# Sums of the quarters of x by adding DMAs, with the first half of x held negative, and a new order at the beginning of a decoder block kernel

## The chip, the cores and the metric

The kernel runs on one core of a Trainium2 chip. A core has TensorE (PE, matrix products into PSUM), VectorE (DVE), ScalarE (ACT), GpSimd (POOL) and SyncE (SP), each with its own instruction queue, and 16 DMA engines that SP, ACT and POOL give work to. The metric is the device time of one execution in microseconds (us), as the median of several runs. Before the change it is 1400.37 us.

## The reference

One decoder block over x of 1024 positions and 1024 channels, in float32. What matters here is its first step: the RMSNorm of x and the combined input projection.

```python
h = rms_norm(x, mix_norm_g[layer])          # x * rsqrt(mean(x*x) + eps) * g
proj = h @ w_in[layer]                      # 1024 x 5888
z_a, q, k, v, gate_logits = jnp.split(proj, splits, axis=-1)
y_a = chunked_spatial_gating(gelu(z_a), ...)
q, k = partial_rope(q), partial_rope(k)     # needs cos and sin of positions
```

Attention, gates, output projection and the convolutional feed-forward follow; the change touches none of them. The inputs are random, positions run from 0 to 1023.

## The kernel before, in words

**Products in parts.** Each float32 operand is split in a high part, rounded by ACT to float32r, and a low part, the difference, made by DVE. A product of two blocks is three matmul passes (high-high, high-low, low-high). A matmul instruction handles 128 inner channels and 512 positions.

**The input projection by Strassen-Winograd.** x is kept transposed: tile `X` has 8 rows of 128 channels (`kt` 0 to 7) by 1024 positions. Its four quarters are A11 (`kt` 0-3, first 512 positions), A12 (`kt` 4-7, first half), A21 (`kt` 0-3, second half) and A22. `quarter(i, j, kt)` names a row of one: `i` the half of positions, `j` the half of channels. Weights come in pairs of 128 columns (`wr` tiles, two per pair). From pair 2 on, each pair is done with seven block products instead of eight, in the order P1, P2, P6, P7, P5, P4, P3 for pair 2. Their left sides are A11, A12, S2, S3, S1, A22 and S4, with

```
S1 = A21 + A22    S2 = S1 - A11    S3 = A11 - A21    S4 = A12 - S2
```

`x_sum` (L442-450) makes them in place in X: S1 and S2 on DVE, S3 and S4 on POOL, one 128x512 row at a time. `parts_of` and `in_left` (L393-419) split them into the arenas R, G0 and G1, where they stay for all pairs. P2 adds to P1's PSUM bank, P4 to P7's and P3 to P5's; the first value has to be copied out before the second product starts. Pair 2 is evicted to tile C2 by `in_product` (L475-523).

**The first two pairs without the sums.** So that TensorE can start before the norm is known, pairs 0 and 1 multiply the raw x (scaled by the channel gains only, `raw_left`, L429-440) with plain products: `product(n, h, i, k)` is pair n, half h of the positions, column tile i, half k of the channels: 12 matmuls. Their results get the norm factor later, when V is turned (`turn_v`, L595-612). `plain_op` splits the weights, `plain_final` evicts.

**The norm.** `load_rows(h)` loads x by rows into C2 and YC, `square_row` squares them on ACT with a running sum, `root` makes the factor on POOL, `diagonal` (L378) writes it on four diagonals on DVE, `spread` multiplies these with ones on TensorE (`rs_bc`), and `scale_x` (L439) scales X in place.

**The rotation tables.** `rot_tables` (L2146) gives a chain of some 50 small DVE steps (run by `some(n)`), two sines, 16 widening copies on ACT (`wide`), and `turns`: transposes on TensorE and evictions into YC.

**Order.** In `beginning()` (L1024-1125) and through the first seven products, ACT, DVE and TensorE run strictly in the order in which the code calls them. POOL and the DMA queues are placed by the scheduler; each queue runs its own list in order. `meanwhile(i)` (L1127) adds work after product i: S3's parts after P1, S1's after P2, S4's after P7, and then X is released and its memory becomes V, into which the turned blocks of pairs 0 to 2 are evicted. `in_ahead` loads weights and prepares operands ahead.

Of the kernel before, what the change touches and what calls it, by code (L numbers as in the profile page):

```python
# [16 lines left out]
ALU = mybir.AluOpType  # L17
# [76 lines left out]
def block_kernel(  # L94
# [48 lines left out]
    def two(arena, row):  # L143
        return arena[:, row, :].rearrange("p (a t) -> p a t", a=2)
# [197 lines left out]
    for k in range(2):  # L342
        ks = slice(k * QK, (k + 1) * QK)
        nc.sync.dma_start(raws[0, 0][:, ks], w_in[0][:, ks])
        load_x(0, range(k * QK, (k + 1) * QK))
    in_load(0, 1)
    in_load(1, 0)
    load_rows(0)
    in_load(1, 1)
    load_x(1, range(KT))  # L350

    nc.vector.memset(mhalf, -0.5)
    nc.vector.memset(ones, 1.0)
# [16 lines left out]
    def root(h):  # L370
        me = small.tile([P, 4], F32, name=f"me_x{h}", tag="me4", bufs=2)
        rs = rss[h] = small.tile([P, 4], F32, name=f"rs_x{h}", tag="rs4", bufs=2)
        nc.gpsimd.tensor_scalar(me, mss[h], 1.0 / D, EPS, ALU.mult, ALU.add)
        nc.gpsimd.tensor_tensor(rs, me, mhalf.to_broadcast([P, 4]), ALU.pow)

    dgs = [C[1][:, i, upper] for i in range(2)]

    def diagonal(h):  # L378
        for b in range(4):
            dg = dgs[h][:, b * P : (b + 1) * P]  # L380
            nc.vector.tensor_scalar(dg, ident, rss[h][:, b : b + 1], None, ALU.mult)

    def spread(h):
        bc = tr_tile(f"rs_bc{h}")
# [5 lines left out]
    def quarter(i, j, kt):  # L390
        return X[:, j * QK + kt, (lower, upper)[i]]

    def in_left(name, kt, src):  # L393

        arena, row = IN_ROWS[name]
        t = left[name, kt] = two(arena, row + kt)
        return (
            lambda: nc.scalar.activation(t[:, 0], src, AF.Copy),
            lambda: nc.vector.tensor_tensor(t[:, 1], src, f32(t[:, 0]), ALU.subtract),
        )  # L400

    def staggered(items, beside=()):

        beside = list(beside)
        late = None
        for first, hi, lo in items:
            first()
            hi()
            if late:
                late()  # L410
            late = lo
            if beside:
                for fn in beside.pop(0):
                    fn()
        late()

    def parts_of(name, i, j):
        staggered((lambda: None, *in_left(name, kt, quarter(i, j, kt))) for kt in range(QK))

    U_ROWS = {(0, 0): (R, 0), (0, 1): (R, 8), (1, 0): (G1, 0), (1, 1): (R, 12)}
    raw_x = {}

    def raw_left(h, kt):
# [12 lines left out]
        xs = x_half(kt, h)  # L438
        nc.vector.scalar_tensor_tensor(xs, xs, chan[:, kt : kt + 1], bc, ALU.mult, ALU.mult)  # L439

    def x_sum(n, kt):
        a11, a12, a21, a22 = (quarter(i, j, kt) for i in range(2) for j in range(2))  # L442
        if n == 1:
            nc.vector.tensor_tensor(a22, a21, a22, ALU.add)
        elif n == 2:
            nc.vector.tensor_tensor(a11, a22, a11, ALU.subtract)
        elif n == 3:
            nc.gpsimd.tensor_tensor(a21, a11, a21, ALU.subtract)
        else:
            nc.gpsimd.tensor_tensor(a12, a12, a11, ALU.subtract)  # L450


    def c_half(n, i, h):
# [84 lines left out]
    def plain_step(n, h, i, k, kt):  # L538

        if (n, h, i) not in plain_banks:  # L540
            name = f"pl_{n}_{h}_{i}"
            plain_banks[n, h, i] = (
                ps_d.tile([P, HALF], F32, name=name, tag="dn") if i else acc_tile(name)
            )
        acc = plain_banks[n, h, i]
        for p, (w, a) in enumerate(PASSES):
            nc.tensor.matmul(  # L547
                acc, plain_ops[n, k, i][:, w, kt, :], raw_x[h, k * QK + kt][:, a, :],
                start=k == 0 and kt == 0 and p == 0,
                stop=k == 1 and kt == QK - 1 and p == 2,  # L550
                skip_group_check=True,
            )

    def plain_final(n, h, i):
        nc.scalar.activation(c_half(n, i, h), plain_banks[n, h, i], AF.Copy)
# [468 lines left out]
    def beginning():  # L1024

        chain, wide, turns = rot_tables(
            nc, lent, [[C[2][:, i, lower], C[2][:, i, upper]] for i in range(2)],
            acc_tile, ident, positions, YC,
        )
# [12 lines left out]

        def raw_parts(h, kt):
            for fn in raw[h, kt]:
                fn()

        def product(n, h, i, k):
            for kt in range(QK):
                plain_step(n, h, i, k, kt)

        warm_up(12)
        some(5)
        for k in range(2):
            weight(0, k, 0)
            for kt in range(k * QK, (k + 1) * QK):
                raw_parts(0, kt)
            product(0, 0, 0, k)
        some(2)
        weight(0, 0, 1)
        weight(0, 1, 1)  # L1060
        some(4)
        weight(1, 0, 0)
        weight(1, 1, 0)
        plain_final(0, 0, 0)
        for k in range(2):
            product(0, 0, 1, k)
        some(10)
        for b in range(4):
            square_row(0, b)
        load_rows(1)  # L1070
        root(0)
        plain_final(0, 0, 1)
        diagonal(0)
        for k in range(2):
            product(1, 0, 0, k)
        bc0 = spread(0)
        weight(1, 0, 1)
        weight(1, 1, 1)
        for kt in range(KT):
            raw_parts(1, kt)  # L1080
            scale_x(0, kt, bc0)
            some(1)
        plain_final(1, 0, 0)
        for b in range(4):
            square_row(1, b)
        root(1)
        for k in range(2):
            product(1, 0, 1, k)
        some(99)
        plain_final(1, 0, 1)  # L1090
        diagonal(1)
        product(0, 1, 0, 0)
        bc1 = spread(1)
        parts_of("A11", 0, 0)
        product(0, 1, 0, 1)
        parts_of("A12", 0, 1)
        for fn in wide:
            fn()
        for kt in range(KT):
            scale_x(1, kt, bc1)  # L1100
        plain_final(0, 1, 0)
        for k in range(2):
            product(0, 1, 1, k)
        plain_final(0, 1, 1)
        parts_of("A22", 1, 1)
        for kt in range(QK):
            x_sum(1, kt)
            x_sum(3, kt)
        in_ahead(0, 9, 2)
        turns[0]()  # L1110
        for k in range(2):
            product(1, 1, 0, k)
        turns[1]()
        plain_final(1, 1, 0)
        turns[2]()
        for k in range(2):
            product(1, 1, 1, k)
        turns[3]()
        plain_final(1, 1, 1)
        staggered(  # L1120
            (lambda kt=kt: x_sum(2, kt), *in_left("S2", kt, quarter(0, 0, kt)))
            for kt in range(QK)
        )
        for kt in range(QK):
            x_sum(4, kt)

    def meanwhile(i):  # L1127
        if i == 0:
            parts_of("S3", 1, 0)
        elif i == 1:  # L1130
            parts_of("S1", 1, 1)
        elif i == 3:
            parts_of("S4", 0, 1)
            x_stack.close()
            zv["pool"] = zv_stack.enter_context(
                tc.tile_pool(name="zvp", bufs=1, reuse_waits="tile")
            )
# [9 lines left out]
    beginning()  # L1147
# [1133 lines left out]
```

## Time and profile before

| | |
|---|---|
| runs | 1398.46, 1401.39, 1400.37 us; median 1400.37 |
| profiled execution | 1402.62 us, span 1400.9 us |
| TensorE busy | 1368.6 us, 98% of the span |
| VectorE, ScalarE, GpSimd busy | 1036.8, 653.5, 314.8 us |
| granted TensorE clock | 0.993 on average |

The span runs from the first to the last recorded instruction; the execution's own time holds a little more around it. Busy times count compute instructions, not waits or DMA issues. In a timeline row stand start, duration, engine, line of the code, operation, what it writes and reads, its shape, how many, and in brackets the idle time before it with what ended it. `pl` are the plain products, `in_P` the Strassen products, `rs_bc` the spreads, `rot` the table transposes and `vt` the turns of V. In a row of DMA issues stand the count, the size of each and the median us from issue to landing.

### The profile page before, as it was taken

The numbers are of one execution on the slowest core, as the hardware profiler recorded it, in microseconds if no ns is written. First come the engines' busy times: TensorE is split into PE (matmuls) and PEld (weight loads), VectorE is DVE, ScalarE is ACT, GpSimd is POOL, SyncE is SP. The second block draws the span as 40 slices with busy tenths as digits, with TensorE's granted clock in tenths as the row PEclk, the third lists the DMA queues.
The fourth block names the chain that finished last, engine by engine and source line by source line (L and its number), as shares of the span: only waits on it lengthen the run. The fifth ranks groups of instructions, "written<-read, shape, count | busy, mean of one in ns | idle before, by whom it ended". The sixth has DMA issues, their size and how long they took to land.

```text
span 1400.9 us, 19244 instructions
## 1 busy us (share of the span) xinstructions
PE 1368.6 (98%) x6434; PEld 1133.3 (81%) x6434; DVE 1036.8 (74%) x1878; ACT 653.5 (47%) x1285; POOL 314.8 (22%) x305
## 2 busy tenths in 40 slices
PE   9789999999999999999999998999999999999997
PEld 7667888888888788888888877888888888888886
DVE  7978677676876987867889877667666667685674
ACT  7573255555553332634646443334333335454444
POOL 0312000000231000120001147555665554000003
PEclk9999999999999999999999999999999999999999
DMA  9014535354435997694842133223333326997563
GB/s 364 13 49 128 174 105 170 106 166 140 137 104 185 324 310 266 199 313 142 285 130 104 38 113 106 105 93 109 108 105 120 115 74 248 380 318 233 195 211 121
DMA packets 142788, 234.92 MB, mean 168 GB/s; under 512 B 13664, under 2 KB 57440, under 8 KB 142688
## 3 DMA queue, kind: packets, MB, share of 16 engines
q1 hardware_dynamic: 141248, 231.53, 49.4%
q10 hardware_dynamic: 1440, 2.16, 0.4%
q8 instruction: 51, 0.84, 0.2%
q14 instruction: 49, 0.40, 0.1%
HBM read 167.77 MB, written 64.29 MB: 166 GB/s over the span
## 4 chain that ended last, share of the span: by engine, by line
PE 83%; DVE 7%; DMA 4%; issue 3%; ACT 2%; POOL 1%; SPq 0%; POOLq 0%; DVEq 0%; ACTq 0%
PE in_P L486 23%; PE uP L1762 19%; PE dn L2016 11%; PE up L1762 8%; PE pa L1234 5%; PE wo_P L1595 4%; PE pl L547 2%; PE pu L827 2%; PE pu L1741 2%; PE pb L1234 2%; DMA wd<-in_w_down_dram 1%; DMA dS<-gS 1%; PE pp L811 1%; DVE G L166 1%; PE sc L772 1%
## 5 line engine op out<-in xcount | busy, mean ns | idle before, releaser
L486 PE MATMUL in_P<-R,G 128*128 128x512 f32 x1008 | 245.7, 396 | 6.1 <-ACT C L506 4.4
L486 PEld LDWEIGHTS in_P<-R,G 128*128 128x128 f32 x1008 | 186.5, 189 | 43.8 <-ACT C L506 4.8
L2016 PE MATMUL dn<-R 128*128 128x512 f32 x924 | 209.6, 389 | 0.0
L2016 PEld LDWEIGHTS dn<-R 128*128 128x128 f32 x924 | 173.5, 188 | 35.9
L165 ACT ACTIVATE G<-wr 128x512 fp32r<-128x512 f32 x126 | 79.0, 629 | 153.3 <-PE in_P L486 113.3
L165 ACT ACTIVATE R<-up 128x512 fp32r<-128x512 f32 x130 | 79.1, 628 | 123.1 <-PE uP L1762 42.4
L1762 PE MATMUL uP<-G,R 128*128 128x512 f32 x504 | 123.1, 393 | 4.6 <-POOL R L166 2.6
L486 PE MATMUL in_P<-G,G 128*128 128x512 f32 x504 | 123.2, 394 | 1.1 <-DVE C L513 0.8
L1762 PE MATMUL uP<-R 128*128 128x512 f32 x504 | 121.4, 390 | 1.0 <-POOL R L166 1.0
L1762 PE MATMUL up<-G,R 128*128 128x512 f32 x504 | 121.2, 391 | 0.0
L1762 PEld LDWEIGHTS uP<-G,R 128*128 128x128 f32 x504 | 95.4, 190 | 25.3 <-POOL R L166 3.0
L1762 PEld LDWEIGHTS uP<-R 128*128 128x128 f32 x504 | 94.8, 188 | 21.2 <-POOL R L166 1.5
L1762 PEld LDWEIGHTS up<-G,R 128*128 128x128 f32 x504 | 94.6, 188 | 20.5
L486 PEld LDWEIGHTS in_P<-G,G 128*128 128x128 f32 x504 | 92.7, 188 | 20.5 <-issue 1.9
L166 DVE TENSOR_TENSOR G<-wr,G 128x512 fp32r<-128x512 f32 x126 | 90.1, 716 | 20.9 <-ACT G L165 20.9
L166 POOL TENSOR_TENSOR R<-up,R 128x512 fp32r<-128x512 f32 x58 | 88.5, 1526 | 75.6 <-ACT R L165 75.6
L165 ACT ACTIVATE R<-db 128x512 fp32r<-128x512 f32 x77 | 48.1, 626 | 56.3 <-PE dn L2016 46.7
L166 DVE TENSOR_TENSOR R<-up,R 128x512 fp32r<-128x512 f32 x72 | 60.7, 845 | 17.0 <-ACT R L165 17.0
L166 DVE TENSOR_TENSOR R<-db,R 128x512 fp32r<-128x512 f32 x77 | 53.8, 703 | 25.7 <-ACT R L165 25.5
L1234 PE MATMUL pa<-R,G 128*128 128x512 f32 x288 | 67.9, 389 | 0.0
L878 POOL TENSOR_TENSOR ld<-ld,w 128x256 f32<-128x256 f32 x16 | 11.2, 718 | 236.7 <-DVE w L866 236.7
L1234 PEld LDWEIGHTS pa<-R,G 128*128 128x128 f32 x288 | 54.1, 188 | 11.2
(273 smaller groups left out, 2469.4 us busy)
## 6 DMA issues: line engine op xcount, KB each, us to landing
wr<-in_w_in_dram SPq DMA_DIRECT2D x45, 512.0 KB, 4.0
up<-in_w_up_dram SPq DMA_DIRECT2D x44, 512.0 KB, 3.5
dA<-gd SPq DMA_DIRECT2D x55, 256.0 KB, 5.1
wd<-in_w_down_dram SPq DMA_DIRECT2D x44, 256.0 KB, 5.6
wT<-wd SPq DMA_DIRECT2D x44, 256.0 KB, 3.3
dS<-gS SPq DMA_DIRECT2D x44, 256.0 KB, 4.2
db<-wT SPq DMA_DIRECT2D x44, 256.0 KB, 4.3
gd<-Y SPq DMA_DIRECT2D x42, 256.0 KB, 2.0
```

The costliest lines, as they stand in the source:

```text
L165: nc.scalar.activation(hi, src, AF.Copy)
L166: fn = lambda: lo_eng.tensor_tensor(lo, src, f32(hi), ALU.subtract)
L486: nc.tensor.matmul(acc, op[:, w, kt, :], left[LEFT[name], kt][:, a, :], start=opened and kt == 0 and i == 0, stop=kt == QK - 1 and i == 2, ...
L547: nc.tensor.matmul(acc, plain_ops[n, k, i][:, w, kt, :], raw_x[h, k * QK + kt][:, a, :], start=k == 0 and kt == 0 and p == 0, stop=k == 1 ...
L772: nc.tensor.matmul(dst, self.qa[:, h, :], keys, start=True, stop=False)
L811: nc.tensor.transpose(pp[:, i * P : (i + 1) * P], self.pr[:, h, s * P : (s + 1) * P], ident)
L827: nc.tensor.matmul(pu[:, h * HD : (h + 1) * HD], self.pT[:, i, :], vt[:, h * HD : (h + 1) * HD], start=i % n == 0, stop=i % n == n - 1,)
L1234: nc.tensor.matmul(acc, unit[a][kt // 4][:, kt % 4, :], two(R, 8 * h + kt)[:, b, :], start=n == 0 and i == 0, stop=n == len(kts) - 1 and i ...
L1595: nc.tensor.matmul(acc, left[LEFT[name], kt][:, a, blk * P : (blk + 1) * P], out_ops[s][:, w, :], start=name not in SHARED and kt == 0 and ...
L1741: nc.tensor.matmul(acc, plain_up[which, k][:, w, kt, :], left[f"A{h + 1}{k + 1}", kt][:, a, :], start=n == 0 and i == 0, stop=n == KT - 1 ...
L1762: nc.tensor.matmul(acc, op[:, w, kt, :], left[LEFT[name], kt][:, a, :], start=opened and kt == 0 and i == 0, stop=kt == QK - 1 and i == 2, ...
L2016: nc.tensor.matmul(accs[blk], dops[s][:, 0, a, blk * P : (blk + 1) * P], dops[s][:, 1, w, :], start=SEQ[j] not in CONTINUES and kt == 0 an ...
```

## The change

- **Adding DMAs.** `x_sum(n, k)` is now one DMA from the POOL queue for two rows of 512 positions on all partitions (512 KB), which adds its source to its target. S1 is made in `Z`, a view of YC: two plain DMAs on the SP queue, inside the loop of `scale_x(1, ...)`, copy A21 there, then A22 is added. S3 is made over A21, S2 over A11, S4 over A12. There are eight adding DMAs. In the built program POOL's list is S1, S3, S1, S3, S2, S2, S4, S4.
- **Sign.** An adding DMA can't subtract, so the first half of X is scaled by the negative factor (`diagonal(0)`). The parts of A11, A12, S3 and S4 are negated when they are split (`NEGATED`), with a scale of -1 on ACT and a multiply-subtract on DVE.
- **Order.** The second half of x is loaded before the rows and before the weights of pair 1. All plain products of pair 0 come first, for both halves of positions, then those of pair 1. Sixteen chain steps stand between pair 1's weight splits and the first diagonal. The second diagonal is made by ACT. Operands of the first four Strassen products are prepared before the last plain products, and the rest of the chain and the sines come after them.
- **Tables.** The widened tables lie in YC, so they wait until S1's parts are made; their transposes run after the fifth product's second turn, in the PSUM banks of the turns of V (`tr_tile`), where they were among the last plain products in the accumulators' banks.
- **Places.** `U_ROWS` moves the raw parts to other rows of the arenas.

The diff, cut to its core:

```diff
     in_load(0, 1)
+    load_x(1, range(KT))
+    load_rows(0)
     in_load(1, 0)
-    load_rows(0)
-    in_load(1, 1)
-    load_x(1, range(KT))
...
     def diagonal(h):
         for b in range(4):
-            dg = dgs[h][:, b * P : (b + 1) * P]
-            nc.vector.tensor_scalar(dg, ident, rss[h][:, b : b + 1], None, ALU.mult)
+            dg, rs = dgs[h][:, b * P : (b + 1) * P], rss[h][:, b : b + 1]
+            if h == 0:
+                nc.vector.tensor_scalar(dg, ident, rs, -1.0, ALU.mult, ALU.mult)
+            else:
+                nc.scalar.activation(dg, ident, AF.Copy, scale=rs)
...
+    NEGATED = ("A11", "A12", "S3", "S4")
     def in_left(name, kt, src):
         arena, row = IN_ROWS[name]
         t = left[name, kt] = two(arena, row + kt)
+        if name in NEGATED:
+            return (
+                lambda: nc.scalar.activation(t[:, 0], src, AF.Copy, scale=-1.0),
+                lambda: nc.vector.scalar_tensor_tensor(
+                    t[:, 1], src, -1.0, f32(t[:, 0]), ALU.mult, ALU.subtract
+                ),
+            )
...
+    Z = YC.rearrange("p i (a t) -> p (i a) t", a=2)
...
-    U_ROWS = {(0, 0): (R, 0), (0, 1): (R, 8), (1, 0): (G1, 0), (1, 1): (R, 12)}
+    U_ROWS = {(0, 0): (R, 4), (0, 1): (R, 12), (1, 0): (G1, 0), (1, 1): (G0, 4)}
...
-    def x_sum(n, kt):
-        a11, a12, a21, a22 = (quarter(i, j, kt) for i in range(2) for j in range(2))
-        if n == 1:
-            nc.vector.tensor_tensor(a22, a21, a22, ALU.add)
-        elif n == 2:
-            nc.vector.tensor_tensor(a11, a22, a11, ALU.subtract)
-        elif n == 3:
-            nc.gpsimd.tensor_tensor(a21, a11, a21, ALU.subtract)
-        else:
-            nc.gpsimd.tensor_tensor(a12, a12, a11, ALU.subtract)
+    def x_sum(n, k):
+        def q(i, j):
+            kt = j * QK + 2 * k
+            return X[:, kt : kt + 2, (lower, upper)[i]]
+        dst, src = {
+            1: (Z[:, 2 * k : 2 * k + 2], q(1, 1)), 3: (q(1, 0), q(0, 0)),
+            2: (q(0, 0), Z[:, 2 * k : 2 * k + 2]), 4: (q(0, 1), q(0, 0)),
+        }[n]
+        nc.gpsimd.dma_start(dst, src, accum_op=ALU.add)
...
         plain_final(0, 0, 0)
+        product(0, 0, 1)
+        for kt in range(KT):
+            raw_parts(1, kt)
+        product(0, 1, 0)
+        plain_final(0, 0, 1)
         for b in range(4):
             square_row(0, b)
         load_rows(1)
+        in_load(1, 1)
         root(0)
+        weight(1, 0, 0)
+        weight(1, 1, 0)
+        plain_final(0, 1, 0)
+        some(16)
         diagonal(0)
+        product(0, 1, 1, (0,))
         bc0 = spread(0)
+        product(0, 1, 1, (1,))
         for kt in range(KT):
             scale_x(0, kt, bc0)
         for b in range(4):
             square_row(1, b)
         root(1)
         diagonal(1)
+        plain_final(0, 1, 1)
+        weight(1, 0, 1)
+        weight(1, 1, 1)
+        product(1, 0, 0)
+        parts_of("A11")
         bc1 = spread(1)
         for kt in range(KT):
             scale_x(1, kt, bc1)
+            if kt in (1, 3):
+                nc.sync.dma_start(Z[:, kt - 1 : kt + 1], X[:, kt - 1 : kt + 1, upper])
+        plain_final(1, 0, 0)
+        product(1, 0, 1)
+        for n, k in ((1, 0), (1, 1), (3, 0), (2, 0), (3, 1), (2, 1)):
+            x_sum(n, k)
+        plain_final(1, 0, 1)
+        parts_of("A12")
+        for k in range(2):
+            x_sum(4, k)
+        product(1, 1, 0)
+        in_ahead(0, 9, 4)
         plain_final(1, 1, 0)
+        some(99)
+        product(1, 1, 1)
         plain_final(1, 1, 1)
+        parts_of("S2")
+        return wide, turns
 
     def meanwhile(i):
         if i == 0:
-            parts_of("S3", 1, 0)
+            parts_of("S3")
         elif i == 1:
-            parts_of("S1", 1, 1)
+            parts_of("S1")
+            parts_of("A22")
+            for fn in wide:
+                fn()
         elif i == 3:
-            parts_of("S4", 0, 1)
+            parts_of("S4")
...
+        elif i == 4:
+            for fn in turns:
+                fn()
```

More of the change, by code (lines that the diff above doesn't have):

```diff
@@ L415, in staggered, with parts_of @@
         late()
-    def parts_of(name, i, j):
-        staggered((lambda: None, *in_left(name, kt, quarter(i, j, kt))) for kt in range(QK))
-    U_ROWS = {(0, 0): (R, 0), (0, 1): (R, 8), (1, 0): (G1, 0), (1, 1): (R, 12)}
+    Z = YC.rearrange("p i (a t) -> p (i a) t", a=2)
+    def parts_of(name, kts=range(QK)):
+        i, j = {"A11": (0, 0), "A12": (0, 1), "A22": (1, 1), "S1": (1, 1), "S2": (0, 0),
+                "S3": (1, 0), "S4": (0, 1)}[name]
+        srcs = [Z[:, kt] if name == "S1" else quarter(i, j, kt) for kt in range(QK)]
+        staggered((lambda: None, *in_left(name, kt, srcs[kt])) for kt in kts)
+    U_ROWS = {(0, 0): (R, 4), (0, 1): (R, 12), (1, 0): (G1, 0), (1, 1): (G0, 4)}
     raw_x = {}
@@ L1026, in beginning @@
         chain, wide, turns = rot_tables(
-            nc, lent, [[C[2][:, i, lower], C[2][:, i, upper]] for i in range(2)],
-            acc_tile, ident, positions, YC,
+            nc, lent, [[YC[:, i, lower], YC[:, i, upper]] for i in range(2)],
+            tr_tile, ident, positions, YC,
         )
@@ L1045, in raw_parts, with product @@
                 fn()
-        def product(n, h, i, k):
-            for kt in range(QK):
-                plain_step(n, h, i, k, kt)
+        def product(n, h, i, ks=(0, 1)):
+            for k in ks:
+                for kt in range(QK):
+                    plain_step(n, h, i, k, kt)
         warm_up(12)
@@ L1056, in beginning @@
                 raw_parts(0, kt)
-            product(0, 0, 0, k)
+            product(0, 0, 0, (k,))
         some(2)
@@ L1060, in beginning @@
         weight(0, 1, 1)
-        some(4)
-        weight(1, 0, 0)
-        weight(1, 1, 0)
         plain_final(0, 0, 0)
-        for k in range(2):
-            product(0, 0, 1, k)
-        some(10)
+        product(0, 0, 1)
[3 more added lines that the diff above has]
+        plain_final(0, 0, 1)
         for b in range(4):
@@ L1070, in beginning @@
         load_rows(1)
+        in_load(1, 1)
         root(0)
-        plain_final(0, 0, 1)
+        weight(1, 0, 0)
+        weight(1, 1, 0)
+        plain_final(0, 1, 0)
+        some(16)
         diagonal(0)
-        for k in range(2):
-            product(1, 0, 0, k)
+        product(0, 1, 1, (0,))
         bc0 = spread(0)
-        weight(1, 0, 1)
-        weight(1, 1, 1)
+        product(0, 1, 1, (1,))
         for kt in range(KT):
-            raw_parts(1, kt)
             scale_x(0, kt, bc0)
-            some(1)
-        plain_final(1, 0, 0)
         for b in range(4):
@@ L1086, in beginning @@
         root(1)
[L1087 to L1090, printed above, removed]
         diagonal(1)
-        product(0, 1, 0, 0)
-        bc1 = spread(1)
[L1094 to L1098, printed above, removed]
+        plain_final(0, 1, 1)
[3 more added lines that the diff above has]
+        parts_of("A11")
+        bc1 = spread(1)
         for kt in range(KT):
             scale_x(1, kt, bc1)
-        plain_final(0, 1, 0)
-        for k in range(2):
[L1103 to L1113, printed above, removed]
+            if kt in (1, 3):
[6 more added lines that the diff above has]
+        parts_of("A12")
+        for k in range(2):
+            x_sum(4, k)
+        product(1, 1, 0)
+        in_ahead(0, 9, 4)
         plain_final(1, 1, 0)
[L1115 to L1118, printed above, removed]
+        some(99)
+        product(1, 1, 1)
         plain_final(1, 1, 1)
[L1120 to L1125, printed above, removed]
+        parts_of("S2")
+        return wide, turns
     def meanwhile(i):
         if i == 0:
-            parts_of("S3", 1, 0)
+            parts_of("S3")
         elif i == 1:
-            parts_of("S1", 1, 1)
+            parts_of("S1")
+            parts_of("A22")
+            for fn in wide:
+                fn()
         elif i == 3:
-            parts_of("S4", 0, 1)
+            parts_of("S4")
             x_stack.close()
@@ L1146, in block_kernel @@
     )
-    beginning()
+    wide, turns = beginning()
     for i, (n, name) in enumerate(in_order):
```

## The prediction

> **What bounds the kernel now.** I read the page first, then the engines in 20 us stretches, then TensorE's timeline. Columns of a stretch: its length, then busy us and count for PE, PEld, DVE, ACT and POOL, then granted clock, DMA share, GB/s.
>
> ```profile
> PE 1368.6 (98%) x6434; PEld 1133.3 (81%) x6434; DVE 1036.8 (74%) x1878; ACT 653.5 (47%) x1285; POOL 314.8 (22%) x305
> ...
> 0.00:20.00 20.00, 17.36 (x74) 13.97 (x75) 14.00 (x37) 14.15 (x24) 0.96 (x14) 1.00 0.91 337
> 20.00:40.00 20.00, 14.44 (x68) 11.77 (x66) 16.16 (x42) 14.10 (x25) 2.45 (x4) 0.92 0.83 323
> 40.00:60.00 20.00, 19.87 (x90) 16.76 (x91) 18.48 (x29) 14.26 (x38) 4.47 (x3) 0.91 0.00 1
> 60.00:80.00 20.00, 13.92 (x54) 10.44 (x53) 16.83 (x20) 9.26 (x16) 8.32 (x6) 0.91 0.00 0
> 80.00:100.00 20.00, 18.04 (x96) 14.37 (x95) 16.30 (x26) 15.00 (x33) 0.00 (x0) 1.00 0.25 79
> 100.00:120.00 20.00, 20.00 (x110) 16.14 (x109) 13.13 (x26) 13.79 (x30) 10.78 (x21) 1.00 0.22 74
> ```
>
> TensorE is busy 98% of the span; of its 32 idle us some 16 lie before 100 us, the only part that the change touches. From there TensorE is full and both programs issue the same work, so a shift there is a shift of the end. My mark is the first product of pair 3, at 97.17.
>
> ```profile
> 11.52 13.84 PE L547 MATMUL pl<-R,G 128*128 128x512 f32 x59 [0.29 <-DVE R L432]
> 25.19 1.05 PE L387 MATMUL rs_bc<-C,ones 128*128 128x128 f32 x8
> ...
> 40.13 2.08 PE L387 MATMUL rs_bc<-C,ones 128*128 128x128 f32 x8 [5.68 <-DVE C L381]
> 41.85 3.87 PE L547 MATMUL pl<-R,G 128*128 128x512 f32 x12
> 45.56 2.88 PE L547 MATMUL pl<-G 128*128 128x512 f32 x12
> ...
> 63.65 3.01 PE L486 MATMUL in_P<-R,G 128*128 128x512 f32 x12
> 71.08 4.60 PE L486 MATMUL in_P<-R,G 128*128 128x512 f32 x12 [4.42 <-ACT C L506]
> ...
> 90.53 0.66 PE L599 MATMUL vt<-ident,C 128*128 128x128 f32 x4 [1.62 <-ACT V L604]
> ...
> 97.17 1.64 PE L486 MATMUL in_P<-R,G 128*128 128x512 f32 x6
> ```
>
> Three waits matter: 5.68 us for the second diagonal, 4.42 us before P2 (P2 adds to P1's bank, so P1's copy must be out first), 1.62 us at the turns of V. The chain of waits tells what held P1's copy: the differences S2 on DVE, and S2's splits, which stand ahead of the copy on ACT.
>
> ```profile
> 68.21 1.68 DVE X L446
> 69.94 0.51 issue
> 70.45 0.58 ACT C L506
> ```
>
> **Durations.** A product costs 13.84/60 = 0.231 us (60 ran, one record is missing); a spread about 0.9. An idle stretch costs more than itself:
>
> ```profile
> 34.00:38.00 4.00, 0.44 (x2) 0.02 (x1) 3.93 (x10) 1.41 (x3) 1.23 (x2) 0.87 0.52 206
> 38.00:42.00 4.00, 1.87 (x9) 1.88 (x10) 3.22 (x14) 2.35 (x6) 0.00 (x0) 0.50 0.01 5
> 42.00:46.00 4.00, 4.00 (x15) 3.24 (x15) 4.00 (x7) 4.00 (x13) 0.00 (x0) 0.78 0.00 0
> ```
>
> After the 5.68 us the clock is at 0.50; from 40.13 to 48.28 a spread and 24 products took 8.15 us where 6.5 is full speed: 1.6 us lost.
>
> ```profile
> 16.04 1.05 ACT L366 ACTIVATE C<-C 128x1024 f32<-128x1024 f32 x1
> 20.68 0.58 ACT L555 ACTIVATE C<-pl 128x512 f32<-128x512 f32 x1
> 25.94 2.62 ACT L431 ACTIVATE R<-X,chan 128x512 fp32r<-128x512 f32 x4
> 40.55 4.26 ACT L398 ACTIVATE R<-X 128x512 fp32r<-128x512 f32 x8
> 44.71 3.29 ACT L2208 ACTIVATE C<-ones 128x128 f32<-128x128 f32 x16
> 89.64 1.57 ACT L604 ACTIVATE V<-vt,rs_x 128x256 f32<-128x256 f32 x4 [1.90 <-DVE G L399]
> ...
> 17.35 0.29 DVE L2163 TENSOR_TENSOR ones<-ones 128x128 f32<-128x128 f32 x1
> 19.72 0.29 DVE L2163 TENSOR_TENSOR ones<-ones 128x128 f32<-128x128 f32 x1
> 41.20 4.91 DVE L399 TENSOR_TENSOR R<-X,R 128x512 fp32r<-128x512 f32 x8 [0.54 <-ACT R L398]
> 46.02 5.35 DVE L439 SCALAR_TENSOR_TENSOR X<-X,chan,rs_bc 128x512 f32<-128x512 f32 x8
> 54.77 4.68 DVE L444 TENSOR_TENSOR X<-X 128x512 f32<-128x512 f32 x4
> ...
> 55.53 6.77 POOL L448 TENSOR_TENSOR X<-X 128x512 f32<-128x512 f32 x4 [20.00 <-DVE X L444]
> ...
> wr<-in_w_in_dram SPq DMA_DIRECT2D x1, 512.0 KB, 7.1
> wr<-in_w_in_dram SPq DMA_DIRECT2D x45, 512.0 KB, 4.0
> C<-in_x_dram SPq DMA_DIRECT2D x4, 512.0 KB, 8.3
> 30.00:34.00 4.00, 4.00 (x19) 3.34 (x18) 4.00 (x10) 3.61 (x8) 0.00 (x0) 1.00 1.03 410
> ```
>
> Per instruction, as start to start: ACT squares of a row 1.16 to 1.25, scaled split 0.64, plain split 0.52, eviction 0.5, widening copy 0.21; DVE difference 0.61, scaling 0.66, step of the rotation chain 2.37/9 = 0.26. Loads run at 410 GB/s when saturated: 0.64 us per X tile, 1.28 per 512 KB.
>
> **The change, part by part.**
>
> *Loads and the first spread.* The X tiles of the second half now follow the load that landed at 6.15 + 7.1 = 13.25, so they land by 18.4 and the first rows by 23.5, and the plain products of the second half come third. TensorE runs 60 products to 25.4 as before, and 12 more to 28.1. The first spread then waits for the first diagonal. On ACT: two weight splits to 14.4, an eviction to 15.0, eight scaled splits to 20.1, an eviction to 20.6, four squares to 25.6, two weight splits to 26.7; on DVE two low parts to 27.4, the 16 chain steps put ahead of the diagonal (4.2) to 31.6, a diagonal to 31.9. TensorE idles 3.8 us (5.68 before) and I charge the 1.6 again. The root is out by 27, so it is the chain that is late, not the load. The diagonal of the second half moves to ACT (four copies of about 0.2 us) and is ready by 36: hidden.
>
> *Plain products.* From 31.9: spread 0.9, 36 products 8.3, spread 0.9 (done 43.6 with the 1.6), 72 products 16.6: 60.2. P1's twelve end at 63.0 (66.66 before). Of this lead 1.8 us is no saving: the 16 transposes of the rotation tables stood here and now come after P5.
>
> *The sums.* Removed are eight DVE and eight POOL instructions; POOL's 1.7 us each stretched DVE's from 0.61 to 1.17 (L444). Added are two 512 KB copies (SP) and eight 512 KB adding DMAs (POOL queue). The second two tiles of X are not needed for the first copy: after two scalings it is issued at 45.0 and lands at 49.0 (4.0, the nearest row). Then the POOL queue, in its listed order, has two adds for S1 and two for S3, then two for S2, each of which needs both kinds landed, then two for S4.
>
> No row shows an adding DMA. Below, it costs what a copy does, 1.28 us of the engines; above, the 5.6 that the 8.3 us of the C rows leave over the fixed part, 4.0 - 1.28 = 2.7. Twice the copy, as the target is read too, is 2.6; POOL's own additions of the same 512 KB take 3.4. I take 3.0, between the two. Four adds land by 49.0 + 2.7 + 12.0 = 63.7, the second add of S2 2.7 + 3.0 later, 69.4. Two splits and P1's copy follow on ACT (1.55): P2 starts at 71.0 after an idle 8.0. Each us on the price moves P2 by 5.
>
> The Trainium skill, page "DMA: Bandwidth & Descriptors", section "Anatomy of one DMA — SWDGE (gpsimd) path", gives a DMA of this queue about 2.0 us plus its bytes over 436 GB/s. By that an add costs 1.2 us of the engines, and the sum would be that of the first rival; no run here shows such a DMA yet.
>
> *P2 to the mark.* 48 products, two turns of V and 1.6 of slow clock take TensorE to 84.6. Next come the rotation transposes, in the banks of the turns, so they wait until ACT has emptied these into V, and V lies where X was, free only after S4's low parts (the 1.90 us of L604 show this wait). After P2 ends at 75.4, ACT has its eviction, eight splits, sixteen widenings and a split to 83.9; DVE then four differences and S4's four scaled low parts to 89.0; V 0.8: 89.8. TensorE idles 5.2. Four transposes, evicted by ACT behind the Gelu of C22, and the slow clock take 3.6: P4 at 93.4; 24 products and five turns 7.7: 101.1. That is 3.9 later than 97.17.
>
> *The negative half* turns eight plain differences into scaled ones (0.05 us each): priced in above, where they count.
>
> **Rivals.**
> 1. *Adds at the rate of a copy (the other side).* Below 1.9 us an add no longer decides: P2 then waits for ACT's own queue. The scalings end at 48.9, A12 and the operands of P1 to P7 on DVE at 58.1, fifteen chain steps at 62.0, sines, an eviction, four splits and the copy: P2 at 65.6, idle 2.6. A wait of 1.62 or 2.6 is short of the whole slow stretch, so the 1.6 goes too: 7.0 earlier, 94.1, 3.1 us faster. For it: plain traffic is nil between 40 and 80 us. Against: the target is read as well. Time 1397.3. Chance 0.25, half of it beyond the 0.2% that a measurement tells from no change.
> 2. *Adds dearer than POOL's.* At 5.0 us P2 moves 10 us: 14 us slower, 1414.5. For it: the rows are 2 KB pieces, three in a chain. Against: X is loaded in pieces as small at 410 GB/s. Chance 0.2.
> 3. *Issue starved by DVE.* POOL has to issue the S2 adds while DVE runs its fifteen chain steps; if an issue waits for the end of these, it costs up to 4: 1408. For it: the stretched L444 shows that POOL and DVE slow each other. Chance 0.1. Beside this: the Trainium skill, "SBUF — State Buffer", section "Who interferes with whom", says that DVE in a 2-port mode keeps GpSimd from writing descriptors; no run here shows it so far.
>
> **How the numbers follow.** The profiled execution took 1402.62 us (span 1400.9), 2.25 above the median 1400.37. The sum is 3.9 us against it, 1406.5; against the median 1404.3. The forecast (add 1.9 to 4.3 us) has 0.45; its own range is 1399 to 1411. Faster: half of rival 1 and a little for a wait that I price too high, 0.2. Same: the other half and the forecast's cheap end, 0.25. Slower: 0.55. The range takes rival 1 with 1 us of error, 1396.5, and rival 2 at 5.0, 1414.5.
>
> **What will show it.** The landing of an adding DMA (1.3 over the fixed 2.7, or 3, or more); TensorE's idle before P2, who releases it (ACT behind the S2 sums) and its length, 8.0; the idle before the first spread, 3.8, released by DVE's diagonal; before the rotation transposes 5.2, released by ACT's V; POOL without compute from 45 to 75; DVE without stretched differences. The prediction is wrong if the adds land by 64, or if TensorE is not dense after the mark.

## The result and the profile after

The changed kernel takes 1418.84 us (median, 1418.01 to 1419.91) where the kernel before takes 1400.88 (1398.46 to 1401.47): a ratio of 1.0131, 95% interval 1.0116 to 1.0146. It is slower by about 18 us; the forecast was 1404.3, within 1396.5 to 1414.5. The profiled execution took 1419.12 us, 16.5 more than the one before (1402.62).

The stretches of the changed kernel, columns as in the prediction:

```profile
PE 1369.8 (97%) x6434; PEld 1135.8 (80%) x6434; DVE 1027.7 (73%) x1866; ACT 656.1 (46%) x1289; POOL 312.1 (22%) x305
...
40.00:60.00 20.00, 20.00 (x93) 16.67 (x93) 16.74 (x29) 9.27 (x17) 2.65 (x2) 1.00 0.51 131
60.00:80.00 20.00, 3.80 (x17) 2.81 (x15) 4.08 (x14) 2.27 (x6) 4.83 (x4) 0.69 0.53 92
```

TensorE's work is the same, but from 60 to 80 us it runs 3.80 of 20, and VectorE and ScalarE (4.08 and 2.27) stand nearly as idle beside it. Half of the DMA engines' time is free too: no engine that does work is the bound there. The timeline of TensorE and ScalarE in the changed kernel:

```profile
32.53 2.08 PE L390 MATMUL rs_bc<-C,ones 128*128 128x128 f32 x8 [5.04 <-DVE C L382]
...
60.92 2.88 PE L504 MATMUL in_P<-R,G 128*128 128x512 f32 x12
83.69 10.45 PE L504 MATMUL in_P<-R,G 128*128 128x512 f32 x36 [19.88 <-ACT C L524]
...
103.09 3.77 PE L2236 MATMUL rot<-ident,YC 128*128 128x128 f32 x16 [5.33 <-ACT V L622]
...
115.13 1.64 PE L504 MATMUL in_P<-R,G 128*128 128x512 f32 x6
...
82.00 1.15 ACT L410 ACTIVATE R<-X 128x512 fp32r<-128x512 f32 x2 [4.23 <-DMA X<-YC]
```

P1 runs at 60.92, P2 only at 83.69, after an idle of 19.88 us that P1's copy ends; the copy stands behind S2's four splits on ScalarE, and the last two of these start at 82.00, when the second add of S2 has landed. The mark, the first product of pair 3, is at 115.13, 17.96 after the kernel before. (1.5 us of that come back behind the mark; where is open.) So the question is why S2 comes at 82.0. POOL's own timeline, and the DMA issues up to 130 us:

```profile
50.05 1.42 POOL L468 DMA_DIRECT2D YC<-X  x1 [15.14 <-DMA YC<-X]
55.60 1.23 POOL L468 DMA_DIRECT2D X<-X  x1 [4.13 <-issue]
60.95 1.20 POOL L468 DMA_DIRECT2D YC<-X  x1 [4.11 <-DVE ones L2174]
66.30 1.22 POOL L468 DMA_DIRECT2D X<-X  x1 [4.14 <-issue]
...
76.92 1.21 POOL L468 DMA_DIRECT2D X<-YC  x1 [4.10 <-DMA X<-YC]
...
X<-X POOLq DMA_DIRECT2D x4, 512.0 KB, 5.0
YC<-X POOLq DMA_DIRECT2D x2, 512.0 KB, 5.2
```

An add is issued in 1.2 us and lands 5.0 to 5.2 us after its issue began, and the next one is issued only then: one every 5.33 us on average, six of them from 50.05 to 82.00. The adds of S3 (the second and fourth rows) wait for no data of the adds before them. The profile gives their 4.1 us of waiting as "issue", which is what it says where it sees no releaser; the others show the same 4.1, with whatever ended last put beside it. No row names what this wait is for; the experiments had to find it.

### The profile page after: what moved, and what is told of

The parts are those of the page before. It is cut to its first block, busy times and chain, and to the rows that moved or that the text cites. A ratio compares the mean times of both kernels' runs of the same rounds, so it can differ in the third digit from the quotient of the medians.

```text
span 1417.4 us, 19246 instructions
## 1 busy us (share of the span) xinstructions
PE 1369.8 (97%) x6434; PEld 1135.8 (80%) x6434; DVE 1027.7 (73%) x1866; ACT 656.1 (46%) x1289; POOL 312.1 (22%) x305
## 4 chain that ended last, share of the span: by engine, by line
PE 83%; DVE 5%; DMA 4%; issue 3%; POOL 2%; ACT 2%; POOLq 0%; SPq 0%; DVEq 0%; ACTq 0%
PE in_P L504 27%; PE uP L1773 19%; PE dn L2027 10%; PE up L1773 8%; PE pa L1245 5%; PE wo_P L1606 4%; PE pu L845 2%; DMA dS<-gS 2%; PE pu L1752 2%; PE pb L1245 2%; PE pl L565 1%; PE pp L829 1%; DMA X<-in_xt_dram 1%; PE sc L790 1%; PE sc L791 1%
```

## The experiments

Three explanations were open: the memory that holds the descriptors of POOL's queue has no room for a second add (1); the queue takes one add at a time in any case (2); an add simply needs its 5 us of transfer (3). The kernel reserves 1,024 bytes a partition for these descriptors, a number in the last function of the file that the change leaves alone.

**Twice the room.**

```diff
-dynamic_dma_scratch_size=1024
+dynamic_dma_scratch_size=2048
-tag="vt", bufs=8
+tag="vt", bufs=7
```

> The memory set aside for the descriptors of POOL's DMA queue is doubled, from 1,024 to 2,048 bytes a partition; the room comes from seven instead of eight buffers for the turned V blocks of the attention. Theory 1, room: one 512 KB add fills that memory by more than half, so the next can only be issued when it has landed. Then the second and fourth adds are issued about 1.3 us after the ones before, the DMA engines (busy some 2.6 us of each 5.3 now) set the pace, the four adds of S1 and S3 land by about 64, those of S2 by about 71, P2 starts near 73 instead of 83.69, and the time is about 1408. Theory 2, the queue takes one add at a time whatever its memory, and theory 3, each add needs its 5 us of transfer: issues still 5.3 us apart, P2 at 83.7, time 1419.

1405.78 us, ratio 1.0042 (1.0026 to 1.0058). POOL's and TensorE's timeline, and a stretch:

```profile
50.77 1.42 POOL L468 DMA_DIRECT2D YC<-X  x1 [16.10 <-DMA YC<-X]
51.73 1.72 POOL L468 DMA_DIRECT2D X<-X  x1
52.46 2.21 POOL L468 DMA_DIRECT2D YC<-X  x1
56.49 1.22 POOL L468 DMA_DIRECT2D X<-X  x1 [1.82 <-issue]
...
72.66 10.04 PE L504 MATMUL in_P<-R,G 128*128 128x512 f32 x36 [8.16 <-ACT C L524]
...
54.00:66.00 12.00, 10.50 (x47) 8.37 (x45) 8.65 (x23) 4.58 (x9) 3.21 (x4) 1.00 1.10 187
```

Three adds are issued back to back; only the fourth waits. With adds always in flight the DMA engines move 187 GB/s, which is 2.8 us for the 524,288 bytes of one add. P2 starts at 72.66, 11 us earlier. Explanation 2 is out, and of 3 what is left is 2.8 us, not 5. (The buffer of V given up for it was not tried alone; the run with 1,088 bytes below gives up none.)

**Adds of half the size.**

```diff
-            kt = j * QK + 2 * k
-            return X[:, kt : kt + 2, (lower, upper)[i]]
+            kt = j * QK + k
+            return X[:, kt : kt + 1, (lower, upper)[i]]
```

> The same sums by sixteen adds of one row (256 KB) instead of eight of two. Theory 1 (room for descriptors): half the descriptors, so two or three are in flight; twelve issues of about 0.8 us and twelve transfers of about 1.3 overlap, S2 lands by about 70, P2 near 72, time about 1407. Theory 2 (one at a time): each of them still pays a fixed part of about 2.7 us beside half the data, some 4 us, twelve in a row take 48 us instead of 32, P2 near 100, time about 1435. Theory 3 (bytes set the price): the same 32 us, time 1419.

1408.29 us, ratio 1.0058 (1.0039 to 1.0078). POOL's and TensorE's timeline:

```profile
49.53 2.88 POOL L468 DMA_DIRECT2D YC<-X  x3 [14.74 <-DVE X L455]
53.32 0.89 POOL L468 DMA_DIRECT2D YC<-X  x1 [0.91 <-DVE R L405]
...
71.49 11.24 PE L504 MATMUL in_P<-R,G 128*128 128x512 f32 x36 [8.22 <-ACT C L524]
```

With the old 1,024 bytes, three one-row adds go out together and the fourth waits. The same bytes in twice as many adds take less time, which neither "one at a time" nor "the bytes" allows.

**Copies in place of adds.**

```diff
-        nc.gpsimd.dma_start(dst, src, accum_op=ALU.add)
+        nc.gpsimd.dma_start(dst, src)
```

> The eight DMAs stay on POOL's queue with their places and waits, but copy instead of adding, so that the sums aren't formed. What is left of the 5.3 us is the price of the queue, what goes is the price of adding. Theory 1: a copy reads only its source and needs fewer descriptors, so two or more may be in flight: second and fourth issued about 1.3 us after the ones before, S2 landed by about 66, P2 near 69, time about 1404. Theory 2: still one after another, each shorter by the read of its target: about 4.0 us, six in 24 us, P2 near 76, time about 1411. Theory 3 (the adding itself is slow): about 1.3 us of data, four landed by 58, time about 1400.

1400.44 us, ratio 0.9999 (0.9989 to 1.0008). POOL's timeline and a stretch, then TensorE's:

```profile
49.25 0.93 POOL L468 DMA_DIRECT2D YC<-X  x1 [14.65 <-DMA YC<-X]
...
50.93 0.72 POOL L468 DMA_DIRECT2D YC<-X  x1
52.94 0.73 POOL L468 DMA_DIRECT2D X<-X  x1 [1.28 <-issue]
...
65.63 10.05 PE L504 MATMUL in_P<-R,G 128*128 128x512 f32 x36 [2.63 <-ACT C L524]
...
84.66 3.77 PE L2236 MATMUL rot<-ident,YC 128*128 128x128 f32 x16 [5.36 <-ACT V L622]
...
96.65 1.66 PE L504 MATMUL in_P<-R,G 128*128 128x512 f32 x6
...
52.00:58.00 6.00, 6.00 (x28) 4.99 (x27) 5.23 (x9) 2.78 (x6) 1.45 (x2) 1.00 0.92 346
```

Three copies fit and the fourth waits, as with the one-row adds. At 346 GB/s a copy takes 1.5 us of the engines, an add 2.8. The time is the one given for explanation 3, and P2 comes earlier than explanation 1 had it. By itself the run doesn't tell the two apart, since a copy is cheaper and also takes less room than an add; the other runs do. S2's splits wait for no DMA here, so it is also the change with sums that cost nothing: the new order by itself, with P1's copy behind these splits, neither gains nor loses.

**A room counted in packets.** A packet is the unit in which the profile counts what a queue moved. POOL's queue from 44 to 95 us in the changed kernel, with one-row adds and with copies (packets, MB, share of the DMA engines):

```profile
q0 software_dynamic: 2176, 4.19, 47.6%
q0 software_dynamic: 2304, 4.20, 48.2%
q0 software_dynamic: 1152, 4.19, 21.6%
```

That is 17 packets on each of 16 engines for one of the eight two-row adds, 9 for one of the sixteen one-row adds and 9 for one of the eight copies. With 1,024 bytes, 17 and 27 packets were in flight and 34 and 36 were not; with 2,048, 51 were and 68 were not. Both fit one packet for each 32 bytes. That makes a sharp forecast: 34 packets, two adds, need 1,088 bytes.

```diff
-dynamic_dma_scratch_size=1024
+dynamic_dma_scratch_size=1088
```

> 64 bytes more for the descriptors, 1,088 a partition instead of 1,024, and nothing else. A two-row add shows as 17 packets on each DMA engine (2,176 in all for eight), a one-row add as 9 (2,304 for sixteen), a copy as 9 (1,152 for eight). With 1,024 bytes one two-row add is in flight, three one-row adds, three copies; with 2,048 three two-row adds. All of this fits a room of 32 packets an engine for 1,024 bytes. If that is the rule, 1,088 bytes hold 34, so exactly two two-row adds: the second is issued some 1.3 us after the first, the third when the first lands, the pace falls from 5.3 to about 2.8 us, P2 starts at 73 to 74, time about 1406. If a place must stay free, or the size only counts in larger steps, the issues stay 5.3 us apart and the time 1419.

1408.76 us, ratio 1.0055 (1.0036 to 1.0074): 64 bytes give back some 10 us. P2 is earlier than expected (71.76), the time 2.8 us longer; its interval overlaps that of the run with 2,048 bytes. POOL's and TensorE's timeline:

```profile
49.27 1.41 POOL L468 DMA_DIRECT2D YC<-X  x1 [14.81 <-DMA YC<-X]
50.23 1.71 POOL L468 DMA_DIRECT2D X<-X  x1
54.83 1.21 POOL L468 DMA_DIRECT2D YC<-X  x1 [2.90 <-DVE G L166]
...
71.76 10.88 PE L504 MATMUL in_P<-R,G 128*128 128x512 f32 x36 [8.77 <-ACT C L524]
```

Two go out together, the third when the first has landed. The limit of 1,024 bytes therefore lies between 27 and 33 packets, that of 1,088 between 34 and 50; that it is exactly a 32nd of the bytes is the simplest rule through them, not more.

**The sums by instructions, in the new order.**

```diff
+    ENG = {1: 'vector', 2: 'vector', 3: 'gpsimd', 4: 'gpsimd'}
...
-        nc.gpsimd.dma_start(dst, src, accum_op=ALU.add)
+            for r in range(2):
+                e.tensor_tensor(dst[:, r], q(1, 0)[:, r] if n == 1 else dst[:, r], src[:, r], ALU.add)
```

The sums of S2 stand just ahead of its parts, those of S4 behind them.

> The new order and signs stay, but the sums are made by instructions again: S1 (into the same place in YC) and S2 on VectorE, S3 and S4 on GpSimd, one row each; the two copies go. It measures what the order is worth without the adding DMAs. If the late S2 is the whole of the loss, VectorE ends the rotation chain near 62, S1's and S2's sums add 5 to 7 us to it, P2 starts at 68 to 70, and the time is 1403 to 1406. If the order itself loses time elsewhere (after P2), it stays above 1410.

1405.42 us, ratio 1.0041 (1.0028 to 1.0055). The timeline of TensorE, ScalarE and POOL:

```profile
72.27 10.37 PE L511 MATMUL in_P<-R,G 128*128 128x512 f32 x36 [9.25 <-ACT C L531]
...
65.61 0.26 ACT L2219 ACTIVATE ones<-ones 128x64 f32<-128x64 f32 x1 [3.28 <-DVE ones L2180]
...
50.01 12.19 POOL L473 TENSOR_TENSOR X<-X 128x512 f32<-128x512 f32 x4 [15.46 <-DVE YC L473]
```

The time is as expected, and 13 us under the changed kernel; P2 comes 2.3 us later than expected. POOL's first row takes 7.09 us, beside instructions of VectorE that keep their time; its other rows take 1.7, and beside them some of VectorE's take 1.67 instead of 0.69. So the chain ends only at 66.5, S2's sums follow it to 71.1, and the splits that wait for these sums stand ahead of P1's copy on ScalarE.

**The first idle place: the chain ahead of the diagonal.**

```diff
-        some(16)
         diagonal(0)
...
             scale_x(0, kt, bc0)
+        some(16)
```

> The sixteen chain steps go from ahead of the first diagonal to behind the eight scalings of the first half. If these steps are what the first spread waits for, the diagonal is made some 4 us earlier (bound next by the fourth row, squared at 25.8), the idle 5.04 falls to about 1, the slow clock behind it goes too, the copies and adds start 4 to 5 us earlier, and as the six adds in a row still set P2, the time is 1413 to 1415. If the rows are what is late, 1418 to 1419.

1416.93 us, ratio 1.0109 (1.0094 to 1.0124). TensorE's timeline:

```profile
27.48 1.16 PE L390 MATMUL rs_bc<-C,ones 128*128 128x128 f32 x8
...
80.79 11.33 PE L504 MATMUL in_P<-R,G 128*128 128x512 f32 x36 [22.89 <-ACT C L524]
```

The 5.04 us are gone whole, so it was the chain. But the time falls by 1.9 (the two intervals overlap), not by 4 or 5: the steps now stand ahead of A11's parts and the second scalings, the first add starts at 47.20 instead of 50.05, and P2 follows 2.9 us earlier. TensorE's lead only makes the idle before P2 longer, 22.89 for 19.88.

**The last idle place: the rotation transposes.**

```diff
             parts_of("A22")
-            for fn in wide:
-                fn()
...
         elif i == 4:
+            for fn in wide:
+                fn()
+        elif i == 5:
             for fn in turns:
```

> The sixteen widening copies go behind S4's parts on ScalarE, and the sixteen rotation transposes behind the sixth product instead of the fifth. If the idle 5.33 before these transposes is the wait for the turns' banks (for ScalarE's V, which waits for S4's low parts), it shrinks: P4's first products run in its place, S4's splits come 3.3 us earlier, and what is left is a wait of 0 to 2 us at a turn of V; time 1413 to 1416. If something else holds them, the idle moves along with the same length: 1419.

1418.91 us, ratio 1.0125 (1.0110 to 1.0141): no change. The timeline of TensorE and ScalarE:

```profile
99.02 1.62 PE L504 MATMUL in_P<-G,G 128*128 128x512 f32 x6 [1.02 <-ACT G L404]
...
107.92 1.41 PE L2237 MATMUL rot<-ident,YC 128*128 128x128 f32 x8 [3.17 <-ACT V L622]
...
95.72 1.15 ACT L165 ACTIVATE G<-wr 128x512 fp32r<-128x512 f32 x2 [1.99 <-DVE wr L286]
```

The idle is cut into pieces of 1.02, 1.62 (at a turn of V) and 3.17, 5.81 together where 5.33 were. Where the widening copies stood, ScalarE now waits 1.99 us for VectorE's weight sum, and S4's splits come only 0.8 us earlier (96.78 for 97.60): most of the copies' 3.3 us had been hidden beside VectorE, whose list is what comes late.

**Cures together.** S1 and S2 on VectorE (so the two copies to YC go), S3 and S4 by adding DMAs, S2's parts behind P1's copy, the chain and the tables as in the two runs above.

```diff
+    ENG = {1: 'vector', 2: 'vector'}
...
-        parts_of("S2")
+        for n in (2, 4):
+            for k in range(2):
+                x_sum(n, k)
         return wide, turns
...
         if i == 0:
+            parts_of("S2")
             parts_of("S3")
```

> Several cures together: S1 and S2 by VectorE, S3 and S4 by adding DMAs (descriptors at 1,024 bytes), S2's parts behind P1's copy, the chain steps behind the first scalings, the tables later as in the run before. If the three idle places of this beginning are understood, none of them is left above 2 us: P2 follows P1 at about 60, P6 waits at most 2 us for S2, and the time is 1392 to 1397, under the kernel before. If VectorE, which gets 8 additions back, becomes what P6 waits for by over 4 us, it is 1399 to 1402.

1400.04 us, ratio 0.9996 (0.9986 to 1.0006): no gain over the kernel before, and above the 1392 to 1397 that I expected. It lies in the range of the other branch, but P2 waits here (4.48), not P6. TensorE's and VectorE's timeline:

```profile
62.78 10.08 PE L511 MATMUL in_P<-R,G 128*128 128x512 f32 x36 [4.48 <-ACT C L531]
...
26.33 1.29 DVE L560 TENSOR_TENSOR G<-wr,G 128x512 fp32r<-128x512 f32 x2 [5.79 <-ACT G L559]
```

From the end of the chain to S4's parts VectorE hardly stops; its last fifteen chain steps stand ahead of S2's sums, which start at 61.38, and of the sines, which hold P1's copy (4.48). At 20 to 26 us it stands idle for 5.79. The next version uses that place.

```diff
         root(0)
+        some(22)
         weight(1, 0, 0)
...
             scale_x(0, kt, bc0)
-        some(16)
+        some(9)
...
         parts_of("A11")
+        some(99)
...
-                after(1 + b // 2, lambda b=b: turn_v(1, C[1], b))
-                after(5 + b // 2, lambda b=b: turn_v(0, C[0], b))
+                after(3 + b // 2, lambda b=b: turn_v(1, C[1], b))
+                after(7 + b // 2, lambda b=b: turn_v(0, C[0], b))
...
-        elif i == 5:
+        elif i == 6:
             for fn in turns:
...
-dynamic_dma_scratch_size=1024
+dynamic_dma_scratch_size=1088
```

> The mixed version with what its trace asked for: the rotation chain goes where VectorE waits anyway (22 steps between the raw parts of the second half and pair 1's low weights, where it stood idle 5.8 us; 9 behind the first scalings; the rest and the sines behind A11's parts), so that no step of it stands ahead of S2's sums; the turns of V come two places later, the rotation transposes after the seventh product; 1,088 bytes for descriptors. If VectorE's list sets this beginning, S2's sums start near 56 instead of 61.4, P2 follows P1 without an idle place above 1 us, S4's low parts end near 76 instead of 81, and the time is 1389 to 1394. If the idle places only move again, 1398 to 1400.

1394.04 us, ratio 0.9946 (0.9931 to 0.9961): faster than both kernels, and at the slow end of what I expected. A wait of 4.82 before P4 is left. And the same with S3 and S4 on POOL:

```diff
-    ENG = {1: 'vector', 2: 'vector'}
+    ENG = {1: 'vector', 2: 'vector', 3: 'gpsimd', 4: 'gpsimd'}
```

> The same but S3 and S4 by GpSimd's instructions instead of adding DMAs (descriptors at 1,024 bytes, no DMA adds anything). If an adding DMA spares VectorE the slowing that GpSimd's additions bring (S1's additions near 1.2 us instead of 0.62, GpSimd 3 us each), this version is 2 to 6 us slower than the one with adding DMAs. If the sums of S3 and S4 are hidden either way, both are within 1.5 us.

1400.31 us, ratio 0.9996 (0.9985 to 1.0006). VectorE and TensorE with adding DMAs:

```profile
52.63 0.69 DVE L277 TENSOR_TENSOR wr<-wr,wr 128x512 f32<-128x512 f32 x1
...
55.96 2.49 DVE L473 TENSOR_TENSOR X<-X,YC 128x512 f32<-128x512 f32 x4
...
57.93 8.45 PE L511 MATMUL in_P<-R,G 128*128 128x512 f32 x36 [0.69 <-ACT C L531]
...
73.92 2.90 PE L511 MATMUL in_P<-G,G 128*128 128x512 f32 x6 [4.82 <-ACT G L404]
```

and with POOL:

```profile
53.13 1.66 DVE L277 TENSOR_TENSOR wr<-wr,wr 128x512 f32<-128x512 f32 x1
...
59.79 4.66 DVE L473 TENSOR_TENSOR X<-X,YC 128x512 f32<-128x512 f32 x4
...
47.16 12.16 POOL L473 TENSOR_TENSOR X<-X 128x512 f32<-128x512 f32 x4 [12.00 <-DVE YC L473]
```

Beside POOL's additions the same instruction of VectorE takes 1.66 us instead of 0.69, and S2's four sums 4.66 instead of 2.49. POOL's four rows are one of 7.08 us and three of 1.7, as in the run with all sums by instructions. Beside adding DMAs no instruction of VectorE is seen slowed: at 52.63 the DMA engines move 187 GB/s for S3's adds, and the instruction takes 0.69. (S2's sums at 55.96 have no add beside them.) In the version with POOL, P6 then waits 3.75 us for S2's low parts. The adds are worth 6.3 us here (1400.31 less 1394.04, with intervals well apart), in a version that makes only S3 and S4 with them.

**P1's copy first, in the changed kernel with 1,088 bytes.** The same move of `parts_of("S2")` as above, with 1,088 bytes.

> The changed kernel with 1,088 bytes for descriptors, and S2's splits behind P1's copy on ScalarE. If P2 only waits because its copy stands behind splits that wait for the adds, P2 runs right after P1, the wait of 8.8 us stands before P6 and is shorter by P2's 2.7; time about 1406 (1408.76 with 1,088 bytes alone). If P2 waits for something else too, no change.

1405.70 us, ratio 1.0040 (1.0026 to 1.0053), 3.1 under the 1408.76 without the move, with intervals that still overlap; the trace shows the move plainly. TensorE's timeline:

```profile
63.83 3.01 PE L504 MATMUL in_P<-R,G 128*128 128x512 f32 x12 [0.69 <-ACT C L524]
```

P2 runs 0.69 us after P1 and needs no sum: it waited only because its copy stood behind splits that waited for the adds. The rest of the wait didn't go where I expected it: before P6 stand only short pieces, and the idle before the rotation transposes grows to 8.78 us (5.31 without the move), so the mark comes 2.4 us earlier.

**A22's parts later.** For the 4.82 us that are left in the best version before P4.

```diff
-            parts_of("A22")
...
+        elif i == 2:
+            parts_of("A22")
```

> The version with all cures, with A22's parts one product later, behind the weight sum and the weight parts of P4. In its trace P4 waits 4.82 us, since its weights are summed on VectorE (L286) only behind S1's and A22's low parts. If the place in VectorE's list is the reason, the weights are ready 2.4 us earlier, the idle shrinks to 1 to 3 us, and the time is 1390 to 1393. If A22's low parts then come just as late, the idle stays at 4 to 5 and the time at 1394.

1395.85 us, ratio 0.9960 (0.9946 to 0.9973), against 0.9946 without it. The intervals of the two versions overlap. TensorE's and VectorE's timeline:

```profile
74.08 2.90 PE L511 MATMUL in_P<-G,G 128*128 128x512 f32 x6 [4.81 <-DVE C L538]
...
73.25 0.68 DVE L538 TENSOR_TENSOR C<-C,in_P 128x512 f32<-128x512 f32 x1
```

The wait stays at 4.81 us. P4's weight sum (L286) is made at 67.59 instead of 69.84 and it does not help, so the weights were not what P4 waited for. The traces name something else: P4 adds to P7's bank, and L538 is the addition on VectorE that takes P7's value out of it. Here it ends at 73.93 and P4 starts at 74.08. Without the move it ends at 73.77 and P4 starts at 73.92; that row names L404, the splits of S4, which P4 doesn't read. In both versions A22's low parts stand ahead of L538 in VectorE's list. No run moves L538, so this is read from the traces and not tested.

## Why the prediction was wrong, step by step

- **Bound and mark: right.** The end follows the mark: 17.96 us there, 16.5 between the profiled executions.
- **Loads and the first spread: right in cause, small in size.** Idle 5.04 for 3.8, ended by VectorE's diagonal; moving the chain removes it.
- **Plain products: right.** P1 at 60.92 for 60.2.
- **The sums: here it failed.** "Four adds land by 49.0 + 2.7 + 12.0 = 63.7" pays the fixed 2.7 us once and lets the four adds follow each other at 3.0. That was taken over from the loads, without a row of POOL's queue behind it. With 1,024 bytes no second add fits, so every add pays its whole 5.33 us: six in a row end at 82.0, not 69.4, and P2 starts at 83.69, not 71.0. These 12.7 us are nearly all of the 14.0 by which the mark was missed (115.13 for 101.1). The rest lies behind P2, which took 31.4 us to the mark for 30.1. Of these 1.3, some 0.5 are the slow clock (36 matmuls took 10.45 us, 8.3 at full speed: 2.1 for the 1.6 charged), and 0.7 lie between the rotation transposes and the mark. In these runs the length of the idle doesn't set this price: the same 36 matmuls took 10.05 us behind 2.63 us of idle, 11.24 behind 8.22.
- **The price itself was near.** 2.8 us of the engines and 5.0 to 5.2 from issue to landing, for 3.0 and 5.7. With room for three adds the run gave P2 at 72.66 and 1405.78 us, for 71.0 and 1404.3: where the adds can follow each other, the sum holds.
- **P2 to the mark: the idle was right (5.33 for 5.2) by luck.** Its working counted the sixteen widening copies (3.4 us) on ScalarE's way to S4. They were mostly hidden beside VectorE, whose weight sum, which the working doesn't name, holds S4's splits nearly as long.
- **Rival 1, adds at the rate of a copy:** the run with copies shows it. P2 at 65.63 after an idle of 2.63, for 65.6 and 2.6; but 1400.44 us, for 1397.3. I let the slow clock go with so short an idle, but the clock is 0.50 behind 2.63 us as well, and the 36 matmuls took 10.05 us for 8.3. That is 1.7 of the 2.5 us by which the mark was late (96.65 for 94.1).

```profile
66.00:68.00 2.00, 2.00 (x6) 1.57 (x5) 1.94 (x5) 2.00 (x5) 0.00 (x0) 0.50 0.00 0
```

- **Rival 2, dearer adds:** its time of 1414.5 came nearest, but that is luck: the transfer is not dear (2.8 us, not 5.0), the adds are alone.
- **Rival 3, issue starved by VectorE:** not seen. The pace is 5.3 to 5.6 us from 50 to 61, where VectorE is busy, and 5.3 from 66 to 77, where it is idle.
- The Trainium skill, page "DMA: Bandwidth & Descriptors", section "Anatomy of one DMA — SWDGE (gpsimd) path", gives about 2.0 us plus the bytes over 436 GB/s, an estimate of 3.2 us for a 512 KB transfer of this queue. The adds took 5.0 to 5.2, the copies 3.7 to 4.3 with others in flight; the measurement decides, and for an add the estimate is too low.

The rivals covered dear and cheap adds and a late issue, but not a queue that holds one add. A question about each new queue was missing: how many of these can be in flight, and what says so?

## What to carry to other kernels

A price for one transfer does not price a row of them: ask what lets the second start before the first has landed. A row of issues at an even distance, with a wait the profile can't name and every engine idle, may be a full queue; halve the pieces or give the descriptors more room, and see whether the distance falls. What stands behind such a transfer on an in-order engine waits with it, needed or not: here P1's copy.

## What the runs showed of the hardware that I had not expected

- POOL's queue holds DMAs by packets: about one packet an engine for each 32 bytes a partition that the program reserves (one add of 17 at 1,024 bytes, two at 1,088, three at 2,048). The Trainium skill, page "DMA: Bandwidth & Descriptors", section "SWDGE vs HWDGE vs iDMA", says that this queue's descriptors lie in rings in a reserved part of SBUF, a pair for each operation. That POOL waits until there is room is what these runs show.
- Adding DMAs moved 187 GB/s, copies in the same place 346: about half, as if the target's read counted in full.
- Issuing costs POOL 1.2 us for an add of two rows, 0.87 for one of one row, 0.72 for a copy of two rows.
- POOL's additions slow some of VectorE's instructions by a factor of 1.9 to 2.4 (2.49 to 4.66, 0.69 to 1.66). Others keep their time, and then POOL's row waits: 7.08 us for one row, 1.7 for the next. Beside adding DMAs at 187 GB/s VectorE's instruction kept its 0.69.
